# Block products in three PSUM banks, a later second root, and two weight sums made by adding transfers

## The chip, the core and the metric

The kernel runs on one core of a Trainium2 chip. The metric is the device time of one execution in microseconds (us), lower is better. TensorE (PE) multiplies, and loads its weights through a queue of its own that the profile shows as PEld; VectorE (DVE) and ScalarE (ACT) do the elementwise work; GpSimd (POOL) takes the powers of the roots, and can issue transfers; SyncE (SP) issues the loads of the weights. Each engine runs its own queue in order and waits for the others through semaphores.

## The reference

One layer of a streaming encoder on 512 positions and 1024 features, in float32:

```python
h = rmsnorm(x, norm_mix_g)
u, v, bg, cg, xs, ga, gb = split(h @ w_in)                 # seven times 1024 columns
v = rmsnorm(gelu(v), norm_v_g)
a = gelu(u) * (w_s[g] (masked, per 128 positions) @ v + b_s[g])
c = bg * causal_dwconv3(cg * xs)
m = sigmoid(ga + b) * (a @ w_proj_a) + sigmoid(gb + b) * (c @ w_proj_b)
x = x + m @ w_out
z = relu(rmsnorm(x, norm_ff_g) @ w_ff1)                    # 1024 -> 4096
x = x + (z * z) @ w_ff2
y = rmsnorm(x, norm_final_g)
```

## The kernel before

**Two halves of a number.** Every operand of a large product is split by `split_into` into a rounded half (`hi`, written by ACT) and the rest (`lo`, written by DVE), and each product is three matmuls: hi by hi, hi by lo, lo by hi. What is computed is held transposed, features on the partitions and the 512 positions along the row.

**Units.** 72 tiles of 128 output features (`unit_matmuls`) take 24 matmuls of 512 columns each: eight k steps of three. They are the u columns, both projections, the b columns, w_out and w_ff2.

**Pairs.** The gates, the c and x columns and w_ff1 are done two tiles at a time (`block_pair`), 32 pairs in all: seven products of quarter blocks (`product`: 12 matmuls of 256 columns each) take the place of eight. Their left sides are raw blocks of the weights (`a1` for P1 and P2, `a22` for D) and sums of blocks (`s31` for E and P7, `s42` for F and P6); the right sides are blocks and sums of the activations, prepared once. A pair's first output is ready after P1, P2, E, P6 and F (`first`). P7 and D, which give the second output (`second`), are put on the list `late`, and a later piece of matmul work calls them through `run_late`. P1, P6, P7 and D add up in one part `A` of a PSUM bank. P2 is written to the other half of the same bank; E and F share a second bank. Seven banks go round.

**Weights.** `load` brings one megabyte at a time on SP's queue into one of two `raw` tiles: two units, or the four blocks of a pair. Splits and sums of the weights are a list of steps (`steps`), taken one at a time by `pump` and at the latest by `need`; four buffers hold split weights. Of a pair the steps are: split a1; `add1` (L218: s31 = the two blocks a11 and a22, each plus a21); split s31; `add2` (L222, L223: s42 from s31 and two blocks); split s42; split a22; load the pair after the next. Both sums have one tile each (`wsum`).

**Stages.** v (16 steps of 12 matmuls of 512 columns, L476), u with the mixing over positions (`mix`), gate A and projection A, the pairs for c and x with the b units, gate B and projection B, w_out, then four chunks of w_ff1 pairs and w_ff2 units. A root 1/sqrt(mean square) is made by `rstd_of`: four one-column matmuls over the summed squares `acc` (L359), one small DVE operation (L350), and one power on POOL (L352); `spread` lays it along the row with four more matmuls (L370). The second root scales the output of the w_ff1 pairs through the tile `Rf` (L819) and stands behind the first of these pairs. Before the last chunk's units the list `late` is emptied (`flush_late`).

The program's order on each queue is not the order of the source text: when the kernel is built, a scheduler lays the instructions out, so the queues are shown below where they matter.

## Time and profile before

| | us |
|---|---|
| median of three runs | 796.01 (795.35 to 796.61) |
| the profiled execution's own time | 796.82 |
| its span, first to last instruction | 795.0 |
| TensorE busy in it | 786.3 |
| VectorE busy | 567.1 |
| ScalarE busy | 362.6 |
| GpSimd busy | 6.3 |

Between the span and the execution's own time lie 1.8 us. Matmuls are pipelined, and the end of one is modelled, so a busy share near 100% hides short stops: what a stop costs is read from the starts of neighbouring matmuls, and from the idle time of the weight-load queue. On the chip 2.4 and 1.2 GHz are the two levels of TensorE's clock; the profile gives the granted clock as a share, 1.00 or 0.50.

### The profile page before, as it was taken

What the parts mean: (1) busy time and instruction counts of PE and PEld (TensorE: products, weight loads), DVE (VectorE), ACT (ScalarE), POOL (GpSimd) and SP (SyncE); (2) the same over time, 40 slices, a digit from 0 to 9 for tenths busy, and PEclk for the clock granted to TensorE, in tenths of its full rate; (3) what the DMA queues carried; (4) which work ended last, traced back from release to release, by engine and by line L of the source; (5) the groups of instructions that cost most, each with busy time, mean ns of one, the idle gap of its engine ahead of it and who ended that gap; (6) DMA issues with size and microseconds to landing.
All of it is one profiled execution on the core that took longest, in us unless ns stands there. A gap on an engine that the chain in (4) does not pass through costs nothing.

```text
span 795.0 us, 11578 instructions
## 1 busy us (share of the span) xinstructions
PE 786.3 (99%) x4798; PEld 703.6 (88%) x4798; DVE 567.1 (71%) x854; ACT 362.6 (46%) x548; POOL 6.3 (1%) x14
## 2 busy tenths in 40 slices
PE   9999999999999999999999999999999999999996
PEld 6888899899899998988888999889988998889886
DVE  7848785556989889766679888556855687557644
ACT  8525354343344443434455566324742365226421
POOL 0000000000000000000000000000000000000000
PEclk9999999999999999999999999999999999999999
DMA  9602113321332323333633023430353025311403
GB/s 343 226 15 97 62 55 106 106 106 54 109 120 92 106 84 129 106 107 106 212 106 106 1 106 109 157 106 1 106 179 140 1 87 178 106 54 54 159 1 106
DMA packets 21444, 83.61 MB, mean 105 GB/s; under 512 B 1936, under 2 KB 2960, under 8 KB 17296
## 3 DMA queue, kind: packets, MB, share of 16 engines
q1 hardware_dynamic: 20384, 81.27, 29.3%
q10 hardware_dynamic: 1008, 1.61, 0.6%
q8 instruction: 37, 0.61, 0.3%
q14 instruction: 15, 0.12, 0.0%
HBM read 80.78 MB, written 2.10 MB: 104 GB/s over the span
## 4 chain that ended last, share of the span: by engine, by line
PE 90%; DVE 4%; DMA 3%; ACT 1%; issue 1%; POOLq 0%; DVEq 0%; ACTq 0%
PE bank L266 16%; PE bank L265 16%; PE bank L267 16%; PE bank L283 12%; PE bank L285 11%; PE bank L284 11%; PE bank L476 6%; DVE wlo L118 2%; DMA raw<-w_pair 1%; DMA raw<-w_main 1%; ACT whi L117 1%; PE bank L530 1%; DMA vec<-vecs 0%; DVE z L118 0%; DVE wsum L218 0%
## 5 line engine op out<-in xcount | busy, mean ns | idle before, releaser
L117 ACT CAST whi<-raw 128x1024 fp32r<-128x1024 f32 (+1 forms) x136 | 128.8, 950 | 185.0 <-PE bank L266 122.8
L118 DVE TENSOR_TENSOR wlo<-raw,whi 128x1024 fp32r<-128x1024 f32 (+1 forms) x136 | 148.6, 1095 | 16.7 <-ACT whi L117 14.9
L266 PE MATMUL bank<-z,whi 128*128 128x512 f32 (+1 forms) x272 | 102.7, 377 | 0.4 <-DVE z L118 0.4
L265 PE MATMUL bank<-z,whi 128*128 128x512 f32 (+1 forms) x272 | 102.8, 378 | 0.0
L267 PE MATMUL bank<-z,wlo 128*128 128x512 f32 (+1 forms) x272 | 102.4, 377 | 0.0
L117 ACT CAST whi<-wsum 128x1024 fp32r<-128x1024 f32 x64 | 67.2, 1050 | 77.0 <-PE bank L266 41.2
L118 DVE TENSOR_TENSOR wlo<-wsum,whi 128x1024 fp32r<-128x1024 f32 x64 | 78.2, 1221 | 26.6 <-ACT whi L117 26.2
L283 PE MATMUL bank<-ft,whi 128*128 128x256 f32 x256 | 73.7, 288 | 0.2
L283 PE MATMUL bank<-xc,whi 128*128 128x256 f32 x256 | 73.2, 286 | 0.2
L284 PE MATMUL bank<-ft,whi 128*128 128x256 f32 x256 | 73.0, 285 | 0.0
L285 PE MATMUL bank<-ft,wlo 128*128 128x256 f32 x256 | 72.5, 285 | 0.0
L285 PE MATMUL bank<-xc,wlo 128*128 128x256 f32 x256 | 72.4, 283 | 0.0
L284 PE MATMUL bank<-xc,whi 128*128 128x256 f32 x256 | 72.4, 283 | 0.0
L837 DVE TENSOR_TENSOR res<-bank,res 128x512 f32<-128x512 f32 x30 | 20.7, 691 | 65.5 <-PE bank L267 65.5
L266 PEld LDWEIGHTS bank<-z,whi 128*128 128x128 f32 x272 | 51.2, 188 | 9.7 <-DVE z L118 0.7
L267 PEld LDWEIGHTS bank<-z,wlo 128*128 128x128 f32 x272 | 51.2, 188 | 9.4
L265 PEld LDWEIGHTS bank<-z,whi 128*128 128x128 f32 x272 | 51.2, 188 | 9.3 <-ACT z L117 0.3
L283 PE MATMUL bank<-fb,whi 128*128 128x256 f32 x192 | 54.9, 286 | 0.0
L283 PE MATMUL bank<-x,whi 128*128 128x256 f32 x192 | 54.5, 284 | 0.0
L284 PE MATMUL bank<-fb,whi 128*128 128x256 f32 x192 | 54.4, 284 | 0.0
L285 PE MATMUL bank<-fb,wlo 128*128 128x256 f32 x192 | 54.3, 284 | 0.0
L284 PE MATMUL bank<-x,whi 128*128 128x256 f32 x192 | 54.3, 283 | 0.0
(157 smaller groups left out, 1799.6 us busy)
## 6 DMA issues: line engine op xcount, KB each, us to landing
raw<-w_main SPq DMA_DIRECT2D x36, 1024.0 KB, 5.0
raw<-w_pair SPq DMA_DIRECT2D x32, 1024.0 KB, 4.8
vraw<-w_v SPq DMA_DIRECT2D x16, 256.0 KB, 5.4
xin<-xT SPq DMA_DIRECT2D x8, 256.0 KB, 5.2
res<-xT SPq DMA_DIRECT2D x8, 256.0 KB, 4.6
out_a<-o SPq DMA_DIRECT2D x4, 256.0 KB, 2.4
wsT<-w_sT ACTq DMA_DIRECT2D x2, 256.0 KB, 4.6
bsb<-b_sb ACTq DMA_DIRECT2D x2, 256.0 KB, 5.0
```

The lines of the kernel that those rows point to most:

```text
L117: nc.scalar.copy(hi, src)
L118: nc.vector.tensor_tensor(lo, src, hi.bitcast(F32), op=ALU.subtract)
L265: nc.tensor.matmul(psum, hi[:, c], act_hi[k][:, cols], start=k == 0, stop=False)
L266: nc.tensor.matmul(psum, hi[:, c], act_lo[k][:, cols], start=False, stop=False)
L267: nc.tensor.matmul(psum, lo[:, c], act_hi[k][:, cols], start=False, stop=k == KT - 1)
L283: nc.tensor.matmul(out, w_hi, x_hi, start=first and sl == 0, stop=False, skip_group_check=True)
L284: nc.tensor.matmul(out, w_hi, x_lo, start=False, stop=False, skip_group_check=True)
L285: nc.tensor.matmul(out, w_lo, x_hi, start=False, stop=sl == KS - 1, skip_group_check=True)
L476: nc.tensor.matmul(vbanks[h][b], xs[k][:, b * P : (b + 1) * P], ws, start=k == 0 and ws is vh and xs is xh, stop=k == KT - 1 and xs is xl,)
L530: nc.tensor.matmul(pm[:, b * P : (b + 1) * P], vt[b][g // 4][:, (g % 4) * P : (g % 4 + 1) * P], wsT[:, g, :], start=True, stop=True,)
L837: nc.vector.tensor_add(res[j], py, res[j])
```

## The change

```diff
--- before.py
+++ after.py
@@ -145,7 +145,7 @@
                 r.rearrange("p (u a) s -> p u (a s)", u=2), w_main[i : i + 2].rearrange("u p f -> p u f")
             )
         else:
-            nc.sync.dma_start(r, w_pair[i])
+            nc.sync.dma_start(r[:, :3, :], w_pair[i, :, :3, :])
         raw_of[n] = r
     def add_operand(src, n=2):
@@ -202,7 +202,16 @@
                 units.append(add_operand(lambda ld=ld, e=e: raw_of[ld][:, 2 * e : 2 * e + 2, :]))
             add_step(lambda ld=ld: load(ld + 2))
-    sums_t = None
+    s31_free, s31_of, built = [], {}, [0]
+    def build():
+        while s31_free and built[0] < w_pair.shape[0]:
+            i, s = built[0], s31_free.pop(0)
+            built[0] += 1
+            s31_of[i] = s
+            nc.gpsimd.dma_start(s.t, w_pair[i, :, 1:3, :])
+            nc.gpsimd.dma_start(s.t, w_pair[i, :, 3:4, :].broadcast_to([P, 2, S]), accum_op=ALU.add)
     def plan_pair():
         ld = len(loads)
@@ -211,22 +220,24 @@
         def raw(a, b):
             return raw_of[ld][:, a:b, :]
-        s31, s42 = sums_t[0].t, sums_t[1].t
-        def add1():
-            nc.vector.tensor_tensor(s31, raw(1, 3), raw(3, 4).broadcast_to([P, 2, S]), op=ALU.add)
+        n = len(pairs)
+        s42 = s42_t.t
+        def done1():
+            s31_free.append(s31_of.pop(n))
+            build()
         def add2():
+            s31 = s31_of[n].t
             nc.vector.tensor_tensor(s42[:, 1, :], s31[:, 1, :], raw(1, 2)[:, 0, :], op=ALU.add)
             nc.vector.tensor_tensor(s42[:, 0, :], s42[:, 1, :], raw(0, 1)[:, 0, :], op=ALU.add)
         tl = {}
         tl["a1"] = add_operand(lambda: raw(0, 2))
-        add_step(add1)
-        tl["s31"] = add_operand(lambda: s31)
+        tl["s31"] = add_operand(lambda: s31_of[n].t)
         add_step(add2)
+        add_step(done1)
         tl["s42"] = add_operand(lambda: s42)
         tl["a22"] = add_operand(lambda: raw(2, 3), n=1)
         add_step(lambda: load(ld + 2))
@@ -292,20 +303,19 @@
-        ba, be = bank(), bank()
-        A, P2, E = ba[:, :N2], ba[:, N2:], be[:, :N2]
+        A, P2, E = (bank()[:, :N2] for _ in range(3))
         c1, c2 = temp("c1"), temp("c2")
         product(p, right, "P1", A, True)
-        product(p, right, "P2", P2, False)
         nc.scalar.copy(c1[:, :N2], A)
+        product(p, right, "P2", P2, True)
         nc.vector.tensor_add(c1[:, :N2], P2, c1[:, :N2])
         run_late()
         product(p, right, "E", E, True)
+        nc.scalar.copy(c2[:, N2:], E)
         product(p, right, "P6", A, False)
-        nc.scalar.copy(c2[:, N2:], E)
+        nc.scalar.copy(c1[:, N2:], A)
         run_late()
         product(p, right, "F", E, False)
-        nc.scalar.copy(c1[:, N2:], A)
         nc.vector.tensor_add(c1[:, N2:], E, c1[:, N2:])
         first(c1)
@@ -379,7 +389,8 @@
             nc.vector.tensor_add(acc, acc, sq)
-    sums_t = slots(2, "wsum")
+    s42_t = Slot("wsum")
+    s31_free.append(Slot("wsum31"))
     plan_units(KT)
     for _ in range(KS):
         plan_pair()
@@ -426,6 +437,8 @@
             vraw_s.append(Slot(f"vraw{i}"))
         t = vraw_s[-1].t[:, i % 2, :]
         nc.sync.dma_start(t, w_v[h, k])
+        if i == KT + 5:
+            build()
         if i == KT + 1 or i == KT + 4:
             load(0 if i == KT + 1 else 1)
         vp = Slot(f"vp{h}{k}", F32R)
@@ -433,8 +446,8 @@
         if h == 0:
             split_into(xh[k], xl[k], xin[k], scale=col(V_GMIX, k))
         split_into(vh, vl, t)
-        if h == 0:
-            sum_squares(acc, xin[k], k)
+        if KS <= i < KS + KT:
+            sum_squares(acc, xin[i - KS], i - KS)
         vparts[i] = vp
     def v_gelu(h, b):
@@ -467,8 +480,10 @@
         if k == 0:
             vbanks[h] = [bank() for _ in range(NB)]
         prep_v(i + V_AHEAD)
-        if i == KT - 1:
+        if i == KT:
             r = rstd_of(acc)
+            for b in range(NB):
+                v_gelu(0, b)
         vp = vparts.pop(i)
         vh, vl = vp.t[:, 0, :], vp.t[:, 1, :]
         for ws, xs in ((vh, xh), (vl, xh), (vh, xl)):
@@ -478,11 +493,8 @@
                     start=k == 0 and ws is vh and xs is xh, stop=k == KT - 1 and xs is xl,
                 )
         vp.give()
-        if i == KT - 1:
-            for b in range(NB):
-                v_gelu(0, b)
-        if KT <= i < KT + NB:
-            v_sq(0, i - KT)
+        if KT < i <= KT + NB:
+            v_sq(0, i - KT - 1)
         if i == KT + 1:
             ws_s = [Slot("wsT", F32, (KT, P)), Slot("bsb", F32, (KT, P))]
             wsT, bsb = (s.t for s in ws_s)
@@ -584,6 +596,8 @@
             for g in range(KT - LAG, KT):
                 mix(g)
             give(*vt_s, *ws_s)
+            s31_free.extend(slots(2, "wsum31"))
+            build()
             ah, al = hi_lo(a_s)
         m1_s.append(Slot(f"m1{p}"))
         pps = []
@@ -801,7 +815,7 @@
         hs = [turn(n) for n in range(2)]
         finish_second(got["r"], hs)
-    wait_rf = []
+    wait_rf, r2 = [], []
     def ff1_pair(p):
         def first(c1):
@@ -815,9 +829,32 @@
         block_pair(n_win + p, right_f, first, second)
         if p == 0:
-            r2 = rstd_of(acc)
-            nc.vector.tensor_copy(Rf, spread(r2))
-            wait_rf.pop()()
+            r2.append(rstd_of(acc))
+            def p7_and_rf(p7=late.pop(0)):
+                p7()
+                nc.vector.tensor_copy(Rf, spread(r2[0]))
+                wait_rf.pop()()
+            late.insert(0, p7_and_rf)
+    def side_by_side(zh, zl):
+        pys, us = [], []
+        for e in range(2):
+            us.append(units[state["next"]])
+            state["next"] += 1
+            pump()
+            need(us[e])
+            pys.append(bank())
+            for k in range(KT - 2):
+                unit_k(pys[e], us[e], k, zh, zl)
+                if k in (0, KT // 2):
+                    run_late()
+        for e in range(2):
+            for k in (KT - 2, KT - 1):
+                unit_k(pys[e], us[e], k, zh, zl)
+            release(us[e])
+        return dict(enumerate(pys))
     done = 0
     for ck in range(NCH):
@@ -825,15 +862,17 @@
         for p in range(done, end):
             ff1_pair(p)
         done = end
-        if ck == NCH - 1:
-            flush_late()
         zh, zl = zip(*[z_tile(ck * CF + i) for i in range(CF)])
         last = ck == NCH - 1
         if last:
             acc2 = [acc[:, :256], acc[:, 256:]]
+        pys = side_by_side(zh, zl) if last else {}
         for j in range(KT - 2 if last else KT):
-            py = bank()
-            unit_matmuls(py, zh, zl)
+            if j in pys:
+                py = pys[j]
+            else:
+                py = bank()
+                unit_matmuls(py, zh, zl)
             nc.vector.tensor_add(res[j], py, res[j])
             if last:
                 for hf in range(2):
```

It does six things.

1. In `block_pair`, A, P2 and E each take a bank of their own, three of the seven instead of two. The copy of A is put right behind P1, the copy of E right behind E, and the copy of A after P6 ahead of F.
2. `add1` is gone from DVE. For each pair POOL issues two transfers from `w_pair`: one writes blocks a11 and a22 into a `wsum31` tile, the second adds block a21 to both (`accum_op`). `build` issues them in pairs as tiles come free; `done1` gives the tile back behind `add2`. There is one tile until the mixing is done, then three.
3. A pair's load leaves the fourth block out: 768 KB instead of 1024.
4. In the v stage the squares of x are planned four steps later and the first root one step later (i = 8 instead of 7), with the four Gelus behind it.
5. The second root's spread and `Rf` move into the first w_ff1 pair's P7, that is into the second pair.
6. Before the last chunk's units `late` is not emptied. The first two of these units do their k steps 0 to 5 side by side, with P7 and D between, and steps 6 and 7 after both (`side_by_side`).

On TensorE, at the second chunk's first w_ff1 pair (`bank_5001` holds A, and P2 in its other half; `bank_5002` holds E; `ft2` is the right side of P6, `fb2` that of F, `bank_5087` belongs to the next pair), the queue before, from the end of E on:

```order
L283 MATMUL bank_5087<-fb110_3736,whi_5019 128x256 [waits Activation_49]
L284 MATMUL bank_5087<-fb110_3736,whi_5019 128x256
L285 MATMUL bank_5087<-fb110_3736,wlo_5020 128x256 [waits DVE_49]
L283 MATMUL bank_5087<-fb110_3736,whi_5019 128x256
L283 MATMUL bank_5002<-fb20_3738,whi_4968 128x256 [waits Activation_49]
L284 MATMUL bank_5002<-fb20_3738,whi_4968 128x256
L285 MATMUL bank_5002<-fb20_3738,wlo_4969 128x256
L283 MATMUL bank_5002<-fb21_3739,whi_4968 128x256
L284 MATMUL bank_5002<-fb21_3739,whi_4968 128x256
L285 MATMUL bank_5002<-fb21_3739,wlo_4969 128x256
L283 MATMUL bank_5002<-fb22_3740,whi_4968 128x256
L283 MATMUL bank_5001<-ft20_3746,whi_4968 128x256 [waits DVE_49]
```

and the same place now, the end of E and the start of P6 (`bank_5048` is A, `bank_5050` is E):

```order
L294 MATMUL bank_5050<-ft13_3785,whi_4985 128x256
L295 MATMUL bank_5050<-ft13_3785,whi_4985 128x256
L296 MATMUL bank_5050<-ft13_3785,wlo_4986 128x256
L294 MATMUL bank_5048<-ft20_3786,whi_5031 128x256 [waits Activation_49]
L295 MATMUL bank_5048<-ft20_3786,whi_5031 128x256
L296 MATMUL bank_5048<-ft20_3786,wlo_5032 128x256 [waits DVE_49]
```

P6 stood behind three matmuls of the next pair and four of F, and waited for DVE; now it follows E directly and waits for ACT, and F stands behind the twelve matmuls of P6.

ScalarE at the same pair, before:

```order
L117 CAST whi_5019<-raw_4889 128x1024 [waits DMAHW3_49,DVE_49,PE_49]
L117 CAST whi_5050<-wsum0_103 128x1024 [waits DVE_49,PE_49,Activation_49]
L300 COPY c1_5003<-bank_5001 128x256 [waits PE_49]
L305 COPY c2_5004<-bank_5002 128x256 [waits PE_49]
L308 COPY c1_5003<-bank_5001 128x256 [waits DVE_49,PE_49]
```

and now:

```order
L117 CAST whi_5085<-raw_4939 128x1024 [waits DMAHW3_49,DVE_49,PE_49]
L309 COPY c1_5051<-bank_5048 128x256 [waits PE_49]
L117 CAST whi_5102<-wsum31_104 128x1024 [waits DMASW5_49,DVE_49,PE_49]
L314 COPY c2_5052<-bank_5050 128x256 [waits PE_49]
L316 COPY c1_5051<-bank_5048 128x256 [waits PE_49]
```

The copy of A went ahead of a weight cast, and no copy waits for DVE any more.

VectorE at the first w_ff1 pair, from the last sum of squares (`acc`) to the copy of the spread root, before:

```order
L379 TENSOR_TENSOR acc_117<-acc_117,sq_4094 128x512 [waits Activation_49]
L118 TENSOR_TENSOR ft13_3745<-T1T3_4084,ft13_3745 128x512 [waits Activation_49]
L118 TENSOR_TENSOR ft23_3749<-T2T4_4085,ft23_3749 128x512 [waits Activation_49]
L301 TENSOR_TENSOR c1_4110<-bank_4108,c1_4110 128x256 [waits Activation_49]
L118 TENSOR_TENSOR wlo_4158<-wsum0_103,whi_4157 128x1024 [waits Activation_49]
L350 TENSOR_SCALAR ms4_4195<-st_4190 128x4 [waits PE_49]
L218 TENSOR_TENSOR wsum0_103<-raw_4112 128x1024 [waits DMAHW3_49,DVE_49]
L369 TENSOR_SCALAR dg4_4199<-ident_81,r4_4197 128x128 [waits Pool_49]
L369 TENSOR_SCALAR dg4_4199<-ident_81,r4_4197 128x128 x3
L309 TENSOR_TENSOR c1_4110<-bank_4109,c1_4110 128x256 [waits PE_49,Activation_49]
L819 COPY R_4097<-bank_4200 128x512 [waits PE_49]
```

and now, to the same operation's first rows on the root (`wsum310` and `wsum311` are sums made by transfers):

```order
L389 TENSOR_TENSOR acc_117<-acc_117,sq_4131 128x512 [waits Activation_49]
L118 TENSOR_TENSOR ft13_3785<-T1T3_4121,ft13_3785 128x512 [waits Activation_49]
L118 TENSOR_TENSOR ft23_3789<-T2T4_4122,ft23_3789 128x512 [waits Activation_49]
L311 TENSOR_TENSOR c1_4148<-bank_4146,c1_4148 128x256 [waits PE_49,Activation_49]
L118 TENSOR_TENSOR wlo_4200<-wsum310_1036,whi_4199 128x1024 [waits Activation_49]
L360 TENSOR_SCALAR ms4_4236<-st_4231 128x4 [waits PE_49]
L319 TENSOR_TENSOR c1_4148<-bank_4147,c1_4148 128x256 [waits PE_49,Activation_49]
L379 TENSOR_SCALAR dg4_4291<-ident_81,r4_4238 128x128 [waits Pool_49]
L379 TENSOR_SCALAR dg4_4291<-ident_81,r4_4238 128x128
L118 TENSOR_TENSOR wlo_4261<-wsum_103,whi_4260 128x1024 [waits Activation_49]
L311 TENSOR_TENSOR c1_4243<-bank_4241,c1_4243 128x256 [waits PE_49,Activation_49]
L379 TENSOR_SCALAR dg4_4291<-ident_81,r4_4238 128x128 x2
```

The add into `wsum0` left the queue; two of the four scalings of the root (`dg4`) now stand behind a split and a copy-add of the second pair.

VectorE in the last part of the mixing, where the steps of the second pair are taken, before:

```order
L118 TENSOR_TENSOR wlo_826<-wsum0_103,whi_825 128x1024 [waits Activation_49]
L535 SCALAR_TENSOR_TENSOR t_m_818<-bank_813,vec_76,bsb_378 128x512 [waits PE_49]
L218 TENSOR_TENSOR wsum0_103<-raw_920 128x1024 [waits DMAHW3_49,DVE_49]
L539 TENSOR_TENSOR t_m_818<-t_m_818,t_u_689 128x512 [waits DVE_49]
L118 TENSOR_TENSOR a2_821<-t_m_818,a2_821 128x512 [waits Activation_49]
L523 TENSOR_TENSOR t_u_855<-bank_824,R_537 128x512 [waits PE_49]
L118 TENSOR_TENSOR wlo_871<-wsum1_104,whi_870 128x1024 [waits Activation_49]
L535 SCALAR_TENSOR_TENSOR t_m_863<-bank_858,vec_76,bsb_378 128x512 [waits PE_49]
L222 TENSOR_TENSOR wsum1_104<-wsum0_103,raw_920 128x512 [waits DVE_49]
L539 TENSOR_TENSOR t_m_863<-t_m_863,t_u_721 128x512 [waits DVE_49]
L223 TENSOR_TENSOR wsum1_104<-wsum1_104,raw_920 128x512 [waits DVE_49]
L118 TENSOR_TENSOR a3_866<-t_m_863,a3_866 128x512 [waits Activation_49]
```

and now:

```order
L118 TENSOR_TENSOR wlo_827<-wsum31_104,whi_826 128x1024 [waits Activation_49]
L547 SCALAR_TENSOR_TENSOR t_m_819<-bank_814,vec_76,bsb_376 128x512 [waits PE_49]
L551 TENSOR_TENSOR t_m_819<-t_m_819,t_u_691 128x512 [waits DVE_49]
L118 TENSOR_TENSOR a2_822<-t_m_819,a2_822 128x512 [waits Activation_49]
L535 TENSOR_TENSOR t_u_856<-bank_825,R_539 128x512 [waits PE_49]
L118 TENSOR_TENSOR wlo_886<-wsum_103,whi_885 128x1024 [waits Activation_49]
L547 SCALAR_TENSOR_TENSOR t_m_864<-bank_859,vec_76,bsb_376 128x512 [waits PE_49]
L233 TENSOR_TENSOR wsum_103<-wsum31_104,raw_937 128x512 [waits DMAHW3_49,DMASW3_49,DVE_49]
L551 TENSOR_TENSOR t_m_864<-t_m_864,t_u_723 128x512 [waits DVE_49]
L234 TENSOR_TENSOR wsum_103<-wsum_103,raw_937 128x512 [waits DVE_49]
L118 TENSOR_TENSOR a3_867<-t_m_864,a3_867 128x512 [waits Activation_49]
```

The sum s42 of the second pair (L222 before, L233 now) stands at the same place in the queue, and now waits for a transfer of POOL (DMASW). POOL's queue at its start, now:

```order
L213 DMA wsum31_104<-w_pair 128x1024
L214 DMA wsum31_104<-w_pair 128x2x512 [waits DMASW0_49]
L362 TENSOR_TENSOR r4_336<-ms4_334,expo_90 128x4 [waits DVE_49,Pool_49]
L362 TENSOR_TENSOR r4_548<-ms4_546,expo_90 128x4 [waits DVE_49,Activation_49,Pool_49]
L213 DMA wsum31_104<-w_pair 128x1024 [waits DMASW1_49,DVE_49]
L214 DMA wsum31_104<-w_pair 128x2x512 [waits DMASW2_49]
L213 DMA wsum310_1036<-w_pair 128x1024 [waits PE_49]
L213 DMA wsum311_1037<-w_pair 128x1024 [waits PE_49]
```

Before, the three powers stood there with nothing between. The second pair's two transfers stand behind the split of the first pair's s31 on DVE, and the second of them behind the landing of the first.

## Rows read from the trace of the kernel before

**Rows 1.** The page: engine, busy us, share of the span, instructions.

```profile
PE 786.3 (99%) x4798; PEld 703.6 (88%) x4798; DVE 567.1 (71%) x854; ACT 362.6 (46%) x548; POOL 6.3 (1%) x14
```

**Rows 2.** Waits of the weight-load queue: us in total, times, longest us.

```profile
PEld bank L283 <- DVE c L301: 2.8, 10, 0.6
PEld bank L283 <- ACT c L305: 1.4, 7, 0.2
```

**Rows 3.** Timeline: start, us, engine, line, operation, [idle before <- releaser]; gate B.

```profile
336.35 1.23 DVE L218 TENSOR_TENSOR wsum<-raw 128x1024 f32<-128x1024 f32 x1 [0.32 <-DMA raw<-w_pair]
...
338.09 0.42 DVE L301 TENSOR_TENSOR c<-bank,c 128x256 f32<-128x256 f32 x1
...
338.57 0.19 PEld L283 LDWEIGHTS bank<-xc,whi 128*128 128x128 f32 x1 [0.56 <-DVE c L301]
```

**Rows 4.** Timeline at the second chunk's first w_ff1 pair.

```profile
544.51 0.19 PEld L283 LDWEIGHTS bank<-fb,whi 128*128 128x128 f32 x1 [0.19 <-ACT c L305]
```

**Rows 5.** Timeline of TensorE around the second root.

```profile
444.64 0.38 PE L283 MATMUL bank<-ft,whi 128*128 128x256 f32 x1
445.38 1.05 PE L359 MATMUL st<-inv_d,acc 128*128 128x1 f32 x8 [0.36 <-DVE acc L379]
...
450.56 0.28 PE L285 MATMUL bank<-fb,wlo 128*128 128x256 f32 x1
450.68 0.28 PE L283 MATMUL bank<-fb,whi 128*128 128x256 f32 x1
```

**Rows 6.** Windows: stretch, us, busy by engine, granted clock, DMA share, GB/s.

```profile
447.00:448.00 1.00, 1.00 (x5) 1.00 (x6) 1.00 (x2) 0.18 (x1) 0.00 (x0) 0.51 0.00 0
...
450.00:450.50 0.50, 0.50 (x4) 0.50 (x4) 0.35 (x2) 0.18 (x1) 0.12 (x1) 0.56 0.00 0
```

**Rows 7.** Timeline of VectorE and GpSimd around the second root.

```profile
444.64 0.69 DVE L379 TENSOR_TENSOR acc<-acc,sq 128x512 f32<-128x512 f32 x1
...
446.78 1.22 DVE L118 TENSOR_TENSOR wlo<-wsum,whi 128x1024 fp32r<-128x1024 f32 x1
...
448.21 1.91 POOL L352 TENSOR_TENSOR r<-ms,expo 128x4 f32<-128x4 f32 x1 [391.91 <-DVE ms L350]
```

**Rows 8.** Timeline at the last chunk's first unit.

```profile
744.27 0.50 PE L265 MATMUL bank<-z,whi 128*128 128x512 f32 x1
744.40 0.69 DVE L118 TENSOR_TENSOR z<-c,z 128x512 fp32r<-128x512 f32 x1
...
745.14 0.50 PE L266 MATMUL bank<-z,whi 128*128 128x512 f32 x1 [0.36 <-DVE z L118]
745.47 0.39 PE L267 MATMUL bank<-z,wlo 128*128 128x512 f32 x1
...
745.70 0.39 PE L265 MATMUL bank<-z,whi 128*128 128x512 f32 x1
```

**Rows 9.** Groups by line and shape: busy us, mean ns | idle before.

```profile
L218 DVE TENSOR_TENSOR wsum<-raw 128x1024 f32<-128x1024 f32 x32 | 39.0, 1220 | 2.8 <-DMA raw<-w_pair 2.6
```

**Rows 10.** DMA issues: out<-in, queue, count, KB each, median us to landing.

```profile
raw<-w_pair SPq DMA_DIRECT2D x32, 1024.0 KB, 4.8
...
out_a<-o SPq DMA_DIRECT2D x4, 256.0 KB, 2.4
```

**Rows 11.** Timeline of VectorE where the second pair's steps are taken.

```profile
87.16 1.23 DVE L118 TENSOR_TENSOR wlo<-wsum,whi 128x1024 fp32r<-128x1024 f32 x1 [0.16 <-ACT whi L117]
...
95.37 0.68 DVE L222 TENSOR_TENSOR wsum<-wsum,raw 128x512 f32<-128x512 f32 x1
...
114.67 0.69 DVE L118 TENSOR_TENSOR a<-t_m,a 128x512 fp32r<-128x512 f32 x1
```

**Rows 12.** Windows, as rows 6, from that add to the last split of `a`.

```profile
95.37:115.36 19.99, 19.99 (x139) 18.58 (x138) 15.94 (x25) 10.73 (x16) 0.00 (x0) 1.00 0.16 53
```

**Rows 13.** The chain that ended last, at the start: start, us, what.

```profile
5.58 19.88 PE bank L476 x84
```

**Rows 14.** Windows, as rows 6, of the start.

```profile
5.00:10.00 5.00, 4.86 (x19) 3.63 (x18) 4.73 (x9) 5.00 (x11) 0.00 (x0) 1.00 1.02 382
```

## The prediction

> **What bounds the kernel now.** I read the page's table of engines first: TensorE is busy for 786.3 of 795.0 us, VectorE for 567.1 [rows 1]. So the time is TensorE's, and a change can win only what TensorE loses in stops and in clock. Its products stay as many as they were. Next came the list of waits of the weight-load queue, where a stop shows best, because a matmul's own bar hides short ones. Two of its lines belong to the block products: 2.8 us in ten waits for VectorE's line 301 (the add that reads P2), and 1.4 us in seven waits for ScalarE's line 305 (the copy of E) [rows 2]. The timeline tells what they are. At 338.57 the weight load of P6 had idled 0.56 us, until the add at 338.09 had ended; the add stood behind the 1.23 us sum of line 218 on VectorE, which itself had waited for a load [rows 3]. P6 doesn't use P2: it waits because P2 lies in the other half of A's bank. At 544.51 the weight load of F idles 0.19 us for the copy of E, because F starts right where E ends [rows 4].
>
> Two single stops remain. At the second root TensorE starts a matmul at 444.64 and its next work, the one-column matmuls of the root, only at 445.38: 0.74 us, where neighbours at full clock are 0.12 apart (450.56 to 450.68) [rows 5]. It waits for the last sum of squares, which ends at 445.33 [rows 7]. Right behind it the granted clock is at its lower level, 1.2 GHz: 0.51 in 447 to 448, and 0.56 in 450.0 to 450.5, so full speed was back at about 450.44 [rows 6]. At the last chunk's first unit starts stand 0.87 us apart (744.27 to 745.14) and then 0.33, where 0.23 is the pace: the unit waits for VectorE's split of z at 744.40 [rows 8].
>
> **The change, part by part.** *Banks and copies.* P2 gets its own bank, so P6 needs only ScalarE's copy of A, which now stands right behind P1, two products ahead. That removes the ten waits, 2.8 us. F now stands behind the twelve matmuls of P6: 12 × 0.12 = 1.44 us of cover for the copy of E, against no cover before, which removes the 1.4 us. What is late next is a free bank: three of seven go to each pair instead of two. A pair lasts 84 matmuls of 0.12, some 10 us, so a bank comes back two pairs later at the earliest and its last reader has several microseconds. I take 4.0 of the 4.2 us; ends 2.0 (half of the waits come back on other releasers) and 4.4.
>
> *Second root.* The root's matmuls stand six matmuls later, 0.72 us, and reach the queue's head at about 445.36, when the sum of squares has just ended (445.33). The stop, 0.74 − 0.12 = 0.62 us, goes. If TensorE no longer stops there, I expect the clock to stay up: the stop at 444.64 stands 2.4 us ahead of the fall. Of 447.0 to 450.44, 3.4 us at half speed, 1.7 us come back. Sum 2.3; ends 0 and 2.8 (with half a microsecond of pace lost around the small matmuls).
>
> *Behind the second root.* GpSimd's power began at 448.21 and took 1.91 us [rows 7]. It now stands behind the issue of the second pair's first transfer, which waits for the split of the first pair's sum on VectorE; that ended at 448.0 (446.78 + 1.22). If the issue keeps GpSimd for a microsecond, the four scalings end near 453. Two of them also stand behind a split of 1.22 us. The spread stands 56 matmuls (6.7 us) behind the root instead of 28, so it wants them at about 452 to 453. I take 0.3 us; ends 0 and 1.5, the wait if the power and the split both come late.
>
> *Last chunk.* TensorE has steps 0 to 5 of two units and two quarter products ahead of the z tiles that it waited for: (0.87 − 0.23) + (0.33 − 0.23) = 0.74 us. No queue is in doubt here; I take 0.7.
>
> *Sums by transfers.* VectorE loses 32 × 1220 ns = 39.0 us [rows 9]. At 71% busy that is off the path, but for the places where line 218 delayed the add of rows 3, counted above. I book no gain for it, nor for the smaller loads. The trace before has no adding transfer. The nearest rows are 2.4 us for a store of 256 KB and 4.8 for a load of 1024 KB, issue to landing [rows 10]; one of the two transfers writes 512 KB. The adding one starts when the first has landed, so both together, T, take from 2 × 2.4 = 4.8 to 2 × 4.8 = 9.6 us. With three tiles they are issued about three pairs ahead, some 30 us, so T is hidden. Two places have less.
>
> The first is the second pair, with one tile. Its transfers start when the split of the first pair's sum has ended, at 87.16 + 1.23 = 88.39. Line 222 needs them; it ran at 95.37 and will wait until 88.39 + T = 93.2 to 98.0. Behind it on VectorE stand the mixing's scalings, the splits of `a` and of projection A's weights. From 95.37 to the end of the last split of `a` (114.67 + 0.69 = 115.36) VectorE was busy for 15.94 us [rows 11, 12], so that split keeps its time while line 222 starts by 115.36 − 15.94 = 99.4, which means T up to 11.0. Both ends lie below. I book 0.2 us for this and other small displacements; ends 0 and 1.
>
> The Trainium skill (DMA: Bandwidth & Descriptors, Anatomy of one DMA — SWDGE (gpsimd) path) gives such a transfer about 2.0 us and its bytes over 436 GB/s. By that the pair of transfers would be an estimated 6.4 us, inside the bounds above; no run here shows a transfer issued by GpSimd.
>
> The second place is the start. The first pair's transfers wait for nothing and meet the loads of x and of v's weights, when the transfer engines are full: share 1.02, 382 GB/s in 5 to 10 us [rows 14]. They take 2 × 512 KB / 382 GB/s = 2.7 us of that capacity. The chain of waits starts with 84 matmuls from 5.58 in 19.88 us, 84 × 0.23 = 19.3, so TensorE is fed almost without a gap there [rows 13]. Its three blocks of four matmuls per step, 12 × 0.23 = 2.8 us, use two loads of 256 KB, which need 1.4 us at 382 GB/s: the loads gain 1.4 us on TensorE with each step, so only a delay in the first step or two is seen. I take 0.5 us; ends 0 and 2.7. The first root, a step later, keeps matmuls of the next half behind it: 0, at most 1.5, about one power of 1.91 us less its cover.
>
> The sum: −4.0 − 2.3 − 0.7 + 0.3 + 0.2 + 0.5 = −6.0 us. Against the profiled execution, 796.8, that is 790.8. This execution was 0.8 above the median of 796.0, so the forecast against the median is 790.0. With the likelier halves of the bounds together the forecast itself reaches from 787.4 (7.9 of gain and next to no new cost, with 0.7 of scatter) to 791.5.
>
> **The rivals.** *A, slower: the adding transfer is much slower than a load.* The price is at the second pair: T − 11.0 us of TensorE. With the other terms the kernel breaks even at T = 17.0, and is slower by over 0.2% (1.6 us, about what a measurement of this kernel can tell from no change) from T = 18.6. At T = 22 it gives 790.0 + 11 = 801. For it: nothing in the trace shows an add made by a transfer, so no row excludes it. Against it: it needs twice the upper bound from rows 10, and transfer engines are nearly idle there, share 0.16 [rows 12]. Chance 0.12, of which 0.09 slower.
>
> *B: the early transfers are paid in full.* 2.7 instead of 0.5 gives 792.2. For it: share 1.02 [rows 14]; against: the growing lead of the loads. Beside it: the Trainium skill (DMA: Bandwidth & Descriptors, Issuing engines are not separate DMA queues) says that transfers of all engines share the same 16 engines and interleave; the share above 1 agrees that nothing is left over there. Chance 0.10.
>
> *C: the waits only change their name (the change doesn't do what it says).* With three banks of seven per pair, P2 of a pair takes the bank of A of two pairs before, whose last reader is VectorE's work on the second output. In the 16 pairs of w_ff1 a wait of 0.25 us each, like the mean of rows 2, would give back 4.0 us: 794.0, and with one of the other terms missing 795 to 796. For it: the wait of 0.56 us shows that VectorE's queue can be late by that much. Against it: VectorE has lost 1.22 us per pair. Chance 0.14, of which 0.10 within 0.2%.
>
> *D: the clock falls at the second root all the same.* The twelve one-column matmuls stay, and a late `Rf` or spread may stop TensorE: 1.7 + 0.6 more gives 792.3. For it: the clock fell just there. Against it: the stop of 0.64 us at 744 is behind work like this one's, and neighbours were soon 0.23 apart [rows 8], the pace of the upper level. Chance 0.12.
>
> **How the numbers follow.** The forecast, 790.0, has 0.52. Faster by over 0.2%: 0.52 + 0.10 (B) + 0.12 (D) + 0.04 (C), 0.78. Within 0.2%: 0.10 (C) + 0.03 (A), 0.13. Slower: 0.09, all of it A. The low end is the forecast's own, 787.4; the high end, 795.6, takes in B, D and most of C, and leaves out A.
>
> **What would show it right or wrong.** In the profile after, the weight-load queue should have no wait for the add that reads P2, and next to none for the copy of E at F; a new line there on line 294 with a VectorE releaser would be C. The granted clock should stay at 1.00 from 445 to 452, or D holds. At the last chunk's first unit starts should be 0.23 apart. VectorE's line 233 near 95 us shows T by its wait for GpSimd's transfer, and the DMA list the landing of each; a stop of TensorE near 115 would be A. Starts of the first matmuls show B: 84 of them should still end near 25.5. The forecast is wrong if two such terms fail together, or if TensorE shows stops at places that had none.

## The result: slower by 1.0%

The changed kernel takes 803.83 us (802.75 to 804.38), the kernel before 795.86 beside it: ratio 1.0098, 95% interval 1.0080 to 1.0115. The forecast was 790.0 with a range of 787.4 to 795.6. The profiled execution of after took 802.75 us with a span of 801.0.

Where the 6.0 us between the two spans come from is read from the weight-load queue first. The list of its waits, after (releaser, us in total, times, longest):

```profile
PEld bank L491 <- ACT vt L454: 5.5, 1, 5.5
PEld bank L491 <- ACT vp L117: 3.7, 2, 2.1
PEld bank L294 <- ACT c L314: 3.7, 4, 1.5
...
PEld bank L294 <- ACT c L324: 1.6, 3, 1.1
```

The first line of [rows 2] is gone: nothing waits for the add that reads P2 any more. But there is a new wait of 5.5 us for the Gelu of v (L454), there are two for the first splits, and in the block products seven for ScalarE's copies. L314 is the copy of E: it is still waited for, in fewer places than before and for up to 1.5 us instead of 0.2. L324 is the copy of P7's result.

**The start.** The chain that ended last, after:

```profile
1.65 6.89 DMA xin<-xT
...
10.45 19.37 PE bank L491 x84
29.82 0.80 PE st L369 x8
```

The second load of x takes 6.89 us (3.3 before), and TensorE, after its first 12 matmuls, starts again only at 10.45. Before, 84 matmuls ran from 5.58 [rows 13], and this piece of the chain followed them:

```profile
25.46 0.79 PE st L359 x8
```

The root now comes after 96 matmuls (12 and 84) instead of 84. Before, it ended at 26.25, and twelve more at 0.23 make about 29.0; after, the same work ends at 30.62. The start costs 1.6 us.

**The first root.** VectorE and GpSimd, and the Gelu on ScalarE, after, in the timeline:

```profile
30.19 0.48 DVE L505 MEMSET wsT<- 64x512 f32 x1 [5.25 <-DMA bsb<-b_sb]
...
33.66 2.36 DVE L118 TENSOR_TENSOR wlo<-raw,whi 128x1024 fp32r<-128x1024 f32 x2
35.93 0.16 DVE L360 TENSOR_SCALAR ms<-st 128x4 f32<-128x4 f32 x1
...
36.24 1.35 POOL L362 TENSOR_TENSOR r<-ms,expo 128x4 f32<-128x4 f32 x1 [25.69 <-DVE ms L360]
...
37.62 2.42 ACT L454 ACTIVATE vt<-bank,r 128x512 f32<-128x512 f32 x4 [3.10 <-POOL r L362]
```

The root's matmuls ended at 30.62, but the small operation on them (L360) stands on VectorE behind a memset that waited 5.25 us for loads of the mixing's constants, and behind the splits queued after it. So it comes at 35.93, the Gelus at 37.62, and TensorE, out of free banks, stops at 32.88 for 5.3 us. Behind the stop the clock is down for a while (stretch, us, busy by engine, granted clock, DMA share, GB/s):

```profile
35.00:40.00 5.00, 1.64 (x4) 1.36 (x5) 4.06 (x10) 2.38 (x4) 1.35 (x1) 0.78 0.63 210
40.00:45.00 5.00, 5.00 (x21) 4.06 (x20) 5.00 (x14) 4.33 (x8) 0.00 (x0) 0.88 0.00 0
```

Six gaps between matmuls are longer by 0.2 to 0.36 us there, 1.4 in all. Stop and clock: 6.6 us.

**The w_ff1 pairs.** ScalarE and TensorE near the end of the first chunk's pairs, after:

```profile
494.71 1.99 ACT L117 CAST whi<-raw 128x1024 fp32r<-128x1024 f32 x2 [2.86 <-DMA raw<-w_main]
496.60 0.37 ACT L314 COPY c<-bank 128x256 f32<-128x256 f32 x1
...
495.47 0.28 PE L296 MATMUL bank<-ft,wlo 128*128 128x256 f32 x1
497.02 0.39 PE L294 MATMUL bank<-fb,whi 128*128 128x256 f32 x1 [1.27 <-ACT c L314]
```

F waits for the copy of E. The copy stands in ScalarE's queue behind two casts of w_ff2's weights, and they waited 2.86 us for their load. The starts give 1.55 where 0.12 is the pace. The same happens at 581 and 666 us, at 590 to the product behind P7 and its copy (L324), and more mildly at 114, for 4.9 us in all.

The sum: 1.6 + 6.6 + 4.9 = 13.1 us lost, and the span is only 6.0 longer, so 7.1 us were won where the forecast put 7.0. In sum the gains came as forecast, and something of 13 us that it had at 1.0 stands against them.

### The profile page after: what moved, and what is told of

It is laid out like the page before. It is cut to its first block, busy times and chain, and to the rows that moved or that the text cites. A ratio compares the mean times of both kernels' runs of the same rounds, so it can differ in the third digit from the quotient of the medians.

```text
span 801.0 us, 11669 instructions
## 1 busy us (share of the span) xinstructions
PE 781.8 (98%) x4798; PEld 702.4 (88%) x4798; DVE 531.9 (66%) x822; ACT 364.2 (45%) x548; POOL 62.7 (8%) x78
## 4 chain that ended last, share of the span: by engine, by line
PE 84%; DMA 7%; DVE 4%; ACT 2%; issue 1%; POOL 0%; DVEq 0%; SPq 0%; POOLq 0%; ACTq 0%
PE bank L276 16%; PE bank L277 16%; PE bank L278 16%; PE bank L294 10%; PE bank L295 10%; PE bank L296 10%; PE bank L491 5%; DMA raw<-w_main 3%; DMA raw<-w_pair 2%; DVE wlo L118 2%; ACT whi L117 1%; DMA xin<-xT 1%; DMA wsum<-w_pair 1%; PE bank L542 1%; DVE wsum L233 0%
## 5 line engine op out<-in xcount | busy, mean ns | idle before, releaser
L118 DVE TENSOR_TENSOR wlo<-raw,whi 128x1024 fp32r<-128x1024 f32 (+1 forms) x136 | 148.2, 1095 | 22.6 <-ACT whi L117 21.5
L294 PE MATMUL bank<-x,whi 128*128 128x256 f32 x192 | 54.5, 284 | 0.4 <-ACT c L314 0.4
L296 PE MATMUL bank<-x,wlo 128*128 128x256 f32 x192 | 54.4, 283 | 0.0
```

The source lines that it names most:

```text
L118: nc.vector.tensor_tensor(lo, src, hi.bitcast(F32), op=ALU.subtract)
L294: nc.tensor.matmul(out, w_hi, x_hi, start=first and sl == 0, stop=False, skip_group_check=True)
L296: nc.tensor.matmul(out, w_lo, x_hi, start=False, stop=sl == KS - 1, skip_group_check=True)
```

## The experiments

Two theories for the losses at the start: the early transfers of the first pair delay the loads (theory 1), or the root one step later is itself what stops TensorE (theory 2). Four kernels cross them.

**The first pair's sum by VectorE (first_by_dve).** The first two lines are in `build`, the others in `plan_pair`; this pair's load is a full one.

```diff
+            if i == 0:
+                continue
+        if n == 0:
+            add_step(lambda: nc.vector.tensor_tensor(s31_of[0].t, raw(1, 3), raw(3, 4).broadcast_to([P, 2, S]), op=ALU.add))
```

> The changed kernel, except that the first pair's s31 is added on VectorE again from a full load of 1024 KB; the other 31 pairs keep their transfers. The changed kernel lost about 2.2 us at its first matmuls, 6.6 us at the first root (a stop of 5.3 us and about 1.4 us of half clock behind it), and 4.9 us in waits of F and P6 for ScalarE's copies. Theory 1 (the early transfers delay the loads of the v stage, VectorE waits for one of them at line 505 ahead of the root's small operation): both the 2.2 and the 6.6 us go, about 795 us. Theory 2 (the root one step later is itself what stops TensorE, behind two more weight splits on VectorE): only the 2.2 us go, the stop at the first root stays at 4 us or more, about 801 us.

795.62 us, ratio 1.0000 (0.9989 to 1.0011). One pair of transfers out of 32 was worth 8 us. On VectorE in this kernel:

```profile
21.47 0.48 DVE L512 MEMSET wsT<- 64x512 f32 x1 [0.74 <-DMA wsT<-w_sT]
...
28.70 0.16 DVE L367 TENSOR_SCALAR ms<-st 128x4 f32<-128x4 f32 x1 [0.89 <-PE st L376]
```

The memset comes at 21.5 instead of 30.2, and the root's operation waits for TensorE, not TensorE for it. The later root is still in place. Theory 1 holds.

**The root where it was (root_back).** The Gelus and their squares move back with it; the diff shows the root and the squares of x alone.

```diff
-        if i == KT:
+        if i == KT - 1:
             r = rstd_of(acc)
-        if KS <= i < KS + KT:
-            sum_squares(acc, xin[i - KS], i - KS)
+        if h == 0:
+            sum_squares(acc, xin[k], k)
```

> The changed kernel with the squares of x and the first root where they were before (i = 7), the transfers kept. Theory 2 (the later root is the cause): the stop of 5.3 us and its half clock go, about 797 us. Theory 1 (the early transfers are the cause): the loads are as late as in the changed kernel, VectorE still waits to about 30 us and the root's small operation comes at 33 to 34 us, so a stop of 3 to 5 us stays, about 800 to 802 us.

803.37 us (1.0102; 1.0085 to 1.0119), as the changed kernel itself. VectorE again stands at the memset:

```profile
29.91 0.48 DVE L506 MEMSET wsT<- 64x512 f32 x1 [6.38 <-DMA bsb<-b_sb]
...
33.37 0.16 DVE L360 TENSOR_SCALAR ms<-st 128x4 f32<-128x4 f32 x1
```

The stop is 4.5 us instead of 5.3: what the later root adds is the two splits more that stand ahead of its operation, under a microsecond, and only because the loads are late. Theory 2 falls.

**All sums by VectorE (sums_back), and the root back as well (both_back).** In both, `add1` and the full loads of before are back, and the other parts stay; in the second the squares and the first root are where they were, too. The diff has the main lines of the first.

```diff
-            nc.sync.dma_start(r[:, :3, :], w_pair[i, :, :3, :])
+            nc.sync.dma_start(r, w_pair[i])
+        def add1():
+            nc.vector.tensor_tensor(s31, raw(1, 3), raw(3, 4).broadcast_to([P, 2, S]), op=ALU.add)
```

> The changed kernel with both weight sums on VectorE and full loads, no adding transfer; the later root, the banks, the later spread and the two units side by side are kept. Theory 1 (everything that was lost hangs on the transfers): no stop at the first root, and the waits for ScalarE's copies at 495, 581, 590 and 666 us go too, about 789 to 790 us. Theory 2: the stop of 5 us at the first root stays, about 796 us. If the waits for the copies come from the new order of banks and copies alone, they stay and add 4 us to either.

> The kernel before with the new banks and copies, the later spread and the two units side by side alone: no transfers, no later root. Both theories: the stops of the kernel before go (4.2 us at P6 and F, 2.3 at the second root with its clock, 0.7 at the last chunk), 788 to 789 us. If the new order of copies is itself the cause of the waits for ScalarE, 792 to 793 us.

788.84 us (0.9914; 0.9899 to 0.9929) and 788.58 us (0.9911; 0.9896 to 0.9926). These are the fastest of all kernels run, faster than before and after. The weight-load queue of sums_back has this left, and no wait in a block product:

```profile
PEld L78 <- issue: 2.2, 8, 0.3
PEld bank L477 <- ACT vp L117: 1.0, 1, 1.0
PEld L78 <- DVE warm L65: 1.0, 1, 1.0
```

So the new banks and copies cause none of the waits for L314 and L324; they need the transfers. The transfers cost 803.8 − 788.8 = 15 us, 8 of it by the first pair's. The squares, the root and the Gelus a step later are worth 0.3 us or nothing.

**The first pair's transfers later (late_start).**

```diff
     nc.vector.tensor_copy(R, Rp)
+    s31_free.append(Slot("wsum31"))
+    nc.vector.tensor_copy(s31_free[0].t[:, 0, 0:1], R[:, 0:1])
+    build()
```

> The changed kernel, except that the first pair's two transfers wait until the first root has been spread (a one-column copy writes to their tile behind R, near 52 us); all 32 pairs keep their transfers. If what costs 8 us at the start is when these two run, and not that they run: both the late first matmuls and the stop at the first root go, 795 to 796 us, as with the first pair on VectorE. If a transfer costs the same wherever it runs: 800 us or more.

796.58 us (1.0004; 0.9990 to 1.0017). The first transfer is issued at 56.60 there, and 7 us come back although all 64 transfers run. What cost was when they ran. A stop of 1.5 us at 31.2 stays: the root's operation comes at 30.54 in this kernel, behind two splits.

**What is left of the loss lies in w_ff1 (ff1_by_dve).** As first_by_dve, with `i == 0 or i >= 16` in place of `i == 0`.

> The changed kernel with the first pair's sum and those of the 16 w_ff1 pairs on VectorE from full loads; 15 pairs keep their transfers. If the 7 us that first_by_dve still loses to sums_back lie in w_ff1 (6 us) and at the second pair (1 us), 789.5 to 790.5 us. If the transfers of the pairs before w_ff1 cost as much each, about 792 us.

790.09 us (0.9933; 0.9918 to 0.9948), 1.25 above sums_back. So the 15 transferred pairs ahead of w_ff1 cost about a microsecond, with one stop of 0.9 us at the second pair, and those of w_ff1 5.5.

**Traffic that nobody waits for (traffic).** sums_back, and for the w_ff1 pairs the two transfers beside it:

```diff
+        nc.vector.tensor_copy(s[:, 0, 0:1], sums_t[1].t[:, 0, 0:1])
+        nc.gpsimd.dma_start(s, w_pair[i, :, 1:3, :])
+        nc.gpsimd.dma_start(s, w_pair[i, :, 3:4, :].broadcast_to([P, 2, S]), accum_op=ALU.add)
```

> sums_back (all sums on VectorE, 788.8 us) and beside it, for the w_ff1 pairs, the same two transfers of GpSimd into two tiles that nothing reads, each started by a one-column copy behind the sum s42 of an earlier pair. If the transfers hurt by taking the transfer engines from SP's loads, ScalarE's casts wait for these loads and the copies behind them are late again: 793 to 796 us. If they hurt because a cast or a sum waits for the transfer's own landing: 789 us, no change.

799.01 us (1.0056; 1.0037 to 1.0074), 10 us above sums_back, more than expected (its pair loads are full ones, so it moves more bytes than the changed kernel); the profiled execution has a span of 793.4, 6.2 above, and where others of its executions lose up to 5 us more isn't shown. Its waits of the weight-load queue:

```profile
PEld bank L292 <- ACT c L322: 4.8, 3, 2.1
...
PEld bank L292 <- ACT c L312: 0.6, 1, 0.6
```

No wait of TensorE, VectorE or ScalarE in this kernel is put down to GpSimd's transfers, and the waits for ScalarE's copies are back. The transfers hurt by running beside the loads; whether they crowd them in the engines or in the memory behind these isn't separated. How, the DMA view shows of the load of w_ff2's first weights, in sums_back (478.5 to 483.3 us) and then in first_by_dve (479.0 to 485.5): queue and kind, packets, MB, share of the 16 engines; issue to landing.

```profile
q1 hardware_dynamic: 272, 1.05, 60.8%
raw<-w_main SPq DMA_DIRECT2D x1, 1024.0 KB, 4.8
```
```profile
q1 hardware_dynamic: 272, 1.05, 42.3%
q0 software_dynamic: 225, 0.69, 40.7%
raw<-w_main SPq DMA_DIRECT2D x1, 1024.0 KB, 6.5
wsum<-w_pair POOLq DMA_DIRECT2D x1, 512.0 KB, 6.4
```

The same load, alone and beside GpSimd's queue: 4.8 and 6.5 us. ScalarE's first cast of these weights waits 0.81 us for it in sums_back and 2.13 in first_by_dve, and the copy of E stands behind the casts.

**Bytes or adding (plain_second).** first_by_dve without the addition.

```diff
-            nc.gpsimd.dma_start(s.t, w_pair[i, :, 3:4, :].broadcast_to([P, 2, S]), accum_op=ALU.add)
+            nc.gpsimd.dma_start(s.t, w_pair[i, :, 3:4, :].broadcast_to([P, 2, S]))
```

> First pair on VectorE as in first_by_dve, and the second transfer of every other pair writes block a21 over the sum instead of adding it, so the sums s31 and s42 and all that follows from them are other numbers; bytes from memory, waits and order stay. If the bytes alone make w_ff1's loads late, 795 to 796 us as first_by_dve; if it is the adding (which holds the transfer engines longer than its bytes say), at least half of the 7 us go, 792 us or less.

793.92 us (0.9982; 0.9962 to 1.0002), executions from 791.2 to 799.1. That lies between the two expectations: in the medians, 1.7 us of the 6.8 that first_by_dve loses to sums_back go. The intervals of the two kernels overlap, so these 1.7 us are not clear of the scatter; the 5.1 us that are left above sums_back are. The queue of GpSimd's transfers, in first_by_dve and then here, as a share of 16 engines' span:

```profile
q0 software_dynamic: 12896, 32.51, 17.8%
```
```profile
q0 software_dynamic: 8928, 32.51, 12.2%
```

For the same 32.51 MB the engines are held for 17.8% of 794.0 us with the adding and 12.2% of 791.5 without: 141 and 97 us, 1.4 us more for each of 31 adding transfers, where a plain one takes 97 / 62 = 1.6. So of the engines' time the bytes take more than the adding. That the adding costs kernel time here is likely, and not shown.

**The copy of E on VectorE (copy_on_dve).** first_by_dve with

```diff
-        nc.scalar.copy(c2[:, N2:], E)
+        nc.vector.tensor_copy(c2[:, N2:], E)
```

> first_by_dve (795.6 us: first pair on VectorE, 31 pairs by transfers) with the copy of E made by VectorE, where it stands ahead of the splits of w_ff2's weights, instead of by ScalarE, where it stands behind two casts that wait for a load. If F stops in w_ff1 because of that place in ScalarE's queue, its three waits there (0.70, 1.18 and 1.41 us) go: 792 to 792.5 us, while the two waits of P7 for ScalarE (0.9 and 1.0 us) stay. If TensorE is held by the late load itself, the stops only move to the next work that needs it: 795 us or more.

802.83 us (1.0121; 1.0076 to 1.0166). The 792 us of the first case did not come; the time lies in the second, 795 or more, and far into it. The waits of the weight-load queue, and VectorE in the second chunk:

```profile
PEld bank L301 <- DVE c L321: 9.9, 10, 1.7
PEld bank L301 <- ACT c L331: 2.8, 3, 1.7
```
```profile
578.96 1.23 DVE L118 TENSOR_TENSOR wlo<-raw,whi 128x1024 fp32r<-128x1024 f32 x1 [2.86 <-ACT whi L117]
580.10 0.42 DVE L321 COPY c<-bank 128x256 f32<-128x256 f32 x1
```

VectorE's queue has the splits of the same weights, which wait for ScalarE's casts and so for the same load. In the first chunk, where the copy happened to stand ahead of them, the stop of first_by_dve at 487 is gone; elsewhere it came back larger, and in others the copy stands behind the sum s42, which waits for a pair's load. So the 3.3 us that the move was to bring did not come, and it cost 7. That a copy with a place behind the late load makes F stop agrees with these rows, but no kernel here takes the copy out of that place throughout.

**Single parts on the kernel before.** `banks_only` has the banks and copies alone, `rf_only` the later spread of the second root alone, `sums_only` the transfers and smaller loads alone; each diff is that part of the change as shown.

> The kernel before with the new banks and copies alone. The forecast's first term was 4.0 us (2.0 to 4.4): 791.6 us from 795.6, with no wait of P6 for the add that reads P2 and none of F for the copy of E. If bank releases take their place (rival C), 794 us or more.

> The kernel before with the second root's spread moved into the second w_ff1 pair alone. The forecast's second term was 2.3 us (0 to 2.8), 0.6 from the stop at 444.6 us and 1.7 from the clock. The banks are the old ones here, and the small stop at P6 of 446.5 us can stay: if the clock stays up all the same, 793.3 us; if it takes the banks as well to keep it up, 795 us.

> The kernel before with the adding transfers and the smaller loads alone (one tile first, then three). If the transfers cost what they cost beside the other parts (803.4 less 788.6 = 14.8 us), 810 us. If the old order of copies bears a late load better, the w_ff1 part (6 us) shrinks and the time is about 804 us; the loss at the start, 8 us, stays in both.

banks_only: 789.30 us (0.9922; 0.9904 to 0.9939), 6.5 us where 4.0 was expected. rf_only: 794.54 us (0.9986; 0.9977 to 0.9996), 1.2 where 2.3 was. With the 0.7 us forecast for the last chunk that is 8.4, more than both_back's 7.0; the intervals (4.9 to 7.6 us and 0.3 to 1.8) leave room for that. For the banks [rows 2] counted 4.2 us of idle time. By the starts of the matmuls, the block products of the kernel before lose 5.1 us outside the stretch of half clock, and those of banks_only 0.6: after a wait the second matmul, too, comes late, 0.22 behind the first instead of 0.12 (338.57 and 338.79). What the rest of the 6.5 is stays open.

The clock is less regular than the forecast took it to be. TensorE at the second root in banks_only, and a window behind it:

```profile
442.06 0.39 PE L283 MATMUL bank<-ft,whi 128*128 128x256 f32 x1
442.81 0.61 PE L358 MATMUL st<-inv_d,acc 128*128 128x1 f32 x4 [0.35 <-DVE acc L378]
```
```profile
444.00:446.00 2.00, 2.00 (x19) 2.00 (x18) 2.00 (x4) 0.71 (x3) 0.36 (x1) 1.00 0.04 8
```

The stop of 0.75 us is still there, and the clock stays at 1.00 behind it, where [rows 6] had 0.51. In rf_only the stop is gone and the clock stays up too. That looks as if the fall of before needed both the stop and the wait at P6 behind it:

```profile
446.50 0.28 PE L285 MATMUL bank<-ft,wlo 128*128 128x256 f32 x1
446.92 0.51 PE L283 MATMUL bank<-ft,whi 128*128 128x256 f32 x1
```

But sums_only has the same stop, 0.74 us, and the same wait, 0.42 from start to start, and no fall:

```profile
458.94 0.39 PE L294 MATMUL bank<-ft,whi 128*128 128x256 f32 x1
459.68 1.05 PE L370 MATMUL st<-inv_d,acc 128*128 128x1 f32 x8 [0.35 <-DVE acc L390]
...
460.80 0.28 PE L296 MATMUL bank<-ft,wlo 128*128 128x256 f32 x1
461.22 0.39 PE L294 MATMUL bank<-ft,whi 128*128 128x256 f32 x1
```
```profile
461.00:463.00 2.00, 1.86 (x16) 1.78 (x16) 1.37 (x3) 0.42 (x2) 0.40 (x1) 1.00 0.03 8
```

What brought the clock down in before is therefore open. It may not even be usual: the profiled execution has a mean granted clock of 0.996, and of the 51 executions of the kernel before that were timed beside the experiments ten have 0.996 or less (796.4 us on average) and 41 have 0.997 to 0.999 (795.4 us).

sums_only: 813.27 us (1.0227; 1.0196 to 1.0258), 17.5 us slower than before, and above both expectations. The median is 2.5 us more than the 15 us that the transfers cost beside the other parts. That the old banks bear late loads worse fits its weight-load queue, which has 4.5 us of waits for the add that reads P2, where [rows 2] had 2.8; but its granted clock is also down once more than that of after, at 0.50 in 142 to 144 us, and by its interval the loss may be 15.6 us.

## Why the prediction was wrong

**What held.** The sum of the three gains: 4.0 + 2.3 + 0.7 = 7.0 us forecast, and both_back is 7.0 us below before. In both_back P6 and F have no wait of their own kind left, and no free bank is late in a block product (rival C did not come). The granted clock of after is 1.00 at the second root, so rival D did not come either. That the sum fits so well is partly luck, because its terms do not: the banks alone gave 6.5 us, above the upper end of 4.4, and the later spread alone 1.2 instead of 2.3. The 1.7 us of the clock were read from one execution and put down to the stop at 444.64; banks_only keeps that stop and the clock, sums_only the stop, the wait and the clock, and most executions of before have a higher mean clock than the profiled one.

**The step that failed first: the start.** The forecast took 0.5 us, at most 2.7, from the bytes over the bandwidth, and reasoned that the v loads gain 1.4 us on TensorE with every step. The late first matmuls cost 1.6 and lie in that range. But it asked only who feeds TensorE. In before the engines stay full past the stretch of [rows 14], at shares of 1.02 to 1.06 up to 25 us, and behind the loads of x and v the first weights and the mixing's constants wait for them. The window from 25 to 30 us, before and then after, shows that these were pushed back: its DMA share was 0.35 and is 0.95.

```profile
25.00:30.00 5.00, 5.00 (x28) 4.24 (x27) 2.60 (x8) 2.64 (x5) 1.02 (x1) 1.00 0.35 127
```
```profile
25.00:30.00 5.00, 5.00 (x26) 4.18 (x25) 0.00 (x0) 2.98 (x5) 0.00 (x0) 1.00 0.95 361
```

In it VectorE is not busy at all: it waits for one of these loads, with the first root's operation behind it. This is the 6.6 us, and there was no term for it, although at the second pair the prediction did name what is queued behind a waiting instruction.

How 2.7 us of transfer time became 8.8 us at the memset (21.4 to 30.2) the traces show. ScalarE issues the loads of the constants, behind its splits of x, and these waited for late loads; before and then after:

```profile
16.04 0.34 ACTq L490 DMA_DIRECT2D wsT<-w_sT  x1
```
```profile
21.84 0.82 ACTq L502 DMA_DIRECT2D wsT<-w_sT  x2
```

So the issue came 5.8 us later, and the second of these loads, which had landed in 4.8 us, took 7.8: 3.0 more. The bytes were also reckoned at too high a rate. From 10 to 15 us, with the adding transfer under way since 9.32, the engines are about as full as before and move 303 GB/s instead of 396; before and then after:

```profile
10.00:15.00 5.00, 5.00 (x24) 4.14 (x23) 5.00 (x10) 5.00 (x11) 0.00 (x0) 1.00 1.06 396
```
```profile
10.00:15.00 5.00, 4.55 (x20) 3.72 (x21) 5.00 (x10) 4.94 (x10) 0.55 (x1) 1.00 1.01 303
```

**The first root: 0, at most 1.5.** Measured 6.6 with the clock, but the later place is not the cause (root_back, sums_back): the number was near the truth, 0.7 us of stop by root_back, and the term missing is the one above.

**T and the second pair.** T was given as 4.8 to 9.6 us. In after the split of the first pair's sum ends at 95.50 + 1.23 = 96.73, and:

```profile
97.03 0.62 POOL L213 DMA_DIRECT2D wsum<-w_pair x1 [32.38 <-DVE wlo L118]
101.15 1.20 POOL L214 DMA_DIRECT2D wsum<-w_pair x1 [3.50 <-DMA wsum<-w_pair]
...
106.59 0.69 DVE L233 TENSOR_TENSOR wsum<-wsum,raw 128x512 f32<-128x512 f32 x1 [2.80 <-issue]
```

T is 9.9 us, just above the upper bound and below the 11.0 from which the last split of `a` would be late; TensorE lost 0.6 us there, near the 0.2 booked (0 to 1). Rival A, the slower side, named the adding transfers' own landing as the mechanism: the side was right and the mechanism wrong.

**The transfers in w_ff1.** "With three tiles, T is hidden" is right: nothing on TensorE's path waits for the sums. The step that failed is that the traffic was booked at nothing once T was hidden. A load of SP that had landed in 4.8 us took 6.5, and ScalarE's queue has casts that wait for such loads ahead of copies that TensorE needs. The 1.44 us of cover for the copy of E were reckoned as if ScalarE could start the copy when E ends. This cost 5.5 us (ff1_by_dve against first_by_dve). The trace before had the sign of it: its copies stood behind casts already, as the order of ScalarE's queue shows, and VectorE's line 218 waited for loads [rows 9].

**Line 218.** The 39.0 us that VectorE lost [rows 9] bought nothing: with them back (sums_back) TensorE has no wait for VectorE in a block product. The prediction had booked no gain for it, rightly.

## What to carry to other kernels

A transfer that nobody waits for still has a price: find the loads that run beside it, see who waits for each, and what stands behind that waiter in its queue. A stretch in which the transfer engines are full has no place for early, unhurried work; the same two transfers cost 8 us when issued from 1.55 us on, and a microsecond or less from 56.60 on. And moving work off an engine that isn't the bound buys only what its queue had been delaying; here a bank of its own for P2 had already taken that.

## What the runs showed of the hardware

An adding transfer of 512 KB took 1.6 + 1.4 = 3.0 us of all 16 engines' time where a plain one took 1.6 (first_by_dve and plain_second). With one under way the full engines moved 303 GB/s at the start of after, and 396 in the same stretch of before. The granted clock fell to 0.50 in the profiled execution of the kernel before, behind a stop of 0.74 us and a wait of 0.42; behind the same two in sums_only it stayed at 1.00.
